# Order of loads, slots and low parts ahead of and inside the first Strassen job of a decoder layer

## The chip, the cores and the metric

The kernel runs on one core of a Trainium2 chip. The metric is the device time of one execution in microseconds; the time of a kernel is the median of its runs. One execution is also recorded by the hardware profiler, and all rows shown come from that one. Engines are named as in the profile: PE is TensorE (PEld its weight loads), DVE is VectorE, ACT is ScalarE, POOL is GpSimd, SP is SyncE, which here only issues DMAs. q1 is the DMA queue that SP issues on, q0 the one of POOL.

## The reference

One layer of a decoder trunk, 512 positions, width 2048, all in float32:

```
h = rms_norm(x)
q, kv, gates, z_a, u|v, z_b, m = split(h @ w_in)          # 2048 x 10800
o_a = sparse_attention(q, kv, gates) * silu(z_a)          # 16 heads of 64, 4 groups
o_b = gelu(u) * (tril(w_s) @ layer_norm(gelu(v)) + b_s) * silu(z_b)
x  += (sigmoid(m_a) * (o_a @ w_up_a) + sigmoid(m_b) * (o_b @ w_up_b)) @ w_out
x  += sigmoid(x @ w_ple_gate) * (p @ w_ple)
out = rms_norm(x)
```

With 512 positions the selection keeps all 8 blocks, so the selected branch is ordinary causal attention, as the window branch is.

## The kernel before

**Matmuls.** Every float32 operand is kept as two parts, a high part (rounded by a copy on ACT, function `high`, L140) and a low part (source minus high part, on DVE, `low`, L146). A product is three matmuls: high by high, high by low, low by high. The parts of h lie in `act_h` and `act_l` (16 k-tiles of 128 by 512 positions).

**Jobs.** A job (L38) is one block of output columns. All jobs form one list, and the generator `gemm` (L312) emits them one after another; `fill(n)` (L406) takes n pieces from it and `finish(name)` (L410) takes pieces until that job is done. Between pieces, other work is emitted (attention, transposes). So the order in which each engine gets its instructions is the order of this Python code, and an instruction that waits holds up those behind it on its engine.

**What runs at each step of a job.** `flush()` (L134) runs the functions in `deferred` (each may put further ones there for the next flush; `later`, L632, puts one two flushes away). `split_to` (L257) makes the high and low weight parts of the step two ahead. `pop()` (L305) takes functions from `background`, `state["pops"]` a step on average. Then come the matmuls, and at the end of a product its `evac`.

**Kinds of job.** "T" and "N" jobs are plain products; a T piece is one k-tile (three matmuls) and a step of it four k-tiles. "S" jobs use Strassen's seven products in Winograd's form on a 2 by 2 split of positions, inner dimension and columns, 2 x 512 columns at a time. Such a job has seven products of four steps; a step has twelve matmuls and four pieces. Most S jobs interleave the products in pairs. Job u (L698) runs them as 1, 2, 5, then 6 and 3 alternating, 7, 4. In the numbering of the code, product 1 needs the first half of h alone, 2 the other half, 5, 6 and 3 need sums of the quarters of h (`hsum_dram`), 7 another one (`h3_dram`, loaded over columns 256 to 511 of `act_h` and `act_l`). Products 1, 6, 7 and 4 add into the same pair of PSUM banks, 5 and 3 into a second pair, 2 has a third (`BANK_OF`, L61).

**What u leaves.** `evac_quad` (L646) copies the results of products 1, 5 and 6 into `keep` tiles on ACT (L656), adds 3, 7 and 2 to them on DVE (L667), and gives each finished quarter to `final_u` (L677: gelu in place on ACT, store by POOL). Product 4 comes from PSUM. `keep` of product 1 uses the tag s1, two slots of the pool quad.

**The stretch around u.** Ahead of it lies the attention (L1083 to L1302), in which the remaining q and za jobs (T) are spread between the attention's own work: `per_period` (L1265) pieces a slot, so that 8 pieces are left at its end. The attention's pool is then closed, and the pools quad and mix open in its place (L1307 to L1310). `load_next` (L224) lets SP ask for u's weights. The rest of za7 follows; its gating (`evac_za`, L530) uses a temporary tile of mix, tag v. Then come, in this order: POOL's loads of the sums for product 3 and of h3 (L1323 to L1328); SP's loads of the spatial-gating weights wn (tag v) and bias bn (tag s1) (L1423 to L1429); `state["pops"] = 1.15` and twelve pieces of u (L1433, L1434); the transpose of bn (L1436) and its copy; four pieces, and twice the transposes of wn, their masking (L1443) into ws (tags g0 and g1), a store and four pieces. Then the four `oa_chunk` lists go into `background`.

**The oa parts.** `oa_chunk(c)` (L1330) prepares the attention's output for the later Strassen job `w_up_a`: 13 entries, one popped at a time. Entry 0 loads two 128x512 tiles (tag v, two slots). `put` takes high and low parts of a tile into one slot each of g0 and g1 and stores them (two to four stores of 128 KB). Entries 3, 6, 9 and 12 are puts; 7 and 8 form sums in place. The chunks must be done when job vn ends, 28 steps after u.

**Keys.** The jobs k00, k01, k10, k11 (`evac_k`, L484) end with four copies on ACT (L489) and, at once, four subtractions on DVE (L491). Meanwhile sums of h are formed in the background (`h_chunk`, L436), each with a high and a low part of its own (tile h_stage).

**Slots.** A pool's tag has a fixed number of slots. A new tile waits until the last reader of the slot's former tile is done, wherever that reader stands in the code.

Of the kernel before, what the change touches and what calls it, by code (L numbers as in the profile page):

```python
# [21 lines left out]
P = 128  # L22
# [42 lines left out]
def kernel(ctx: ExitStack, tc: tile.TileContext, x, p, norm_g, w_in,  # L65
# [418 lines left out]
    def evac_k(b, a):  # L484
        def f(ps):
            g0, g1 = kk(b, 2 * a), kk(b, 2 * a + 1)
            lo_r, up_r = slice(0, 64), slice(64, 128)
            for dst, srow, g in ((lo_r, lo_r, g0), (up_r, up_r, g1), (up_r, lo_r, g0), (lo_r, up_r, g1)):
                nc.scalar.copy(ob_h[dst, g], ps[srow])  # L489
            for dst, srow, g in ((lo_r, lo_r, g0), (up_r, up_r, g1), (up_r, lo_r, g0), (lo_r, up_r, g1)):  # L490
                nc.vector.tensor_tensor(out=ob_l[dst, g], in0=ps[srow], in1=ob_h[srow, g].bitcast(F32),  # L491
                                        op=ALU.subtract)
        return f
# [151 lines left out]

    def evac_quad(final, place=None, tiles=True):  # L646

# [3 lines left out]
        def e(p, ps):  # L651
            if p in "156":
                tag, pool, bufs = {"1": ("s1", quad["pool"], 2), "5": ("hi", stream, 4), "6": ("lo", stream, 3)}[p]
                keep[p] = [pool.tile([P, 512], F32, tag=tag, name="keep" + p, bufs=bufs) for _ in range(2)]
                for t in range(2):
                    nc.scalar.copy(keep[p][t], ps[t])  # L656
            elif p in "372":
                other, row, c = {"3": ("6", 0, 512), "7": ("5", 2, 512), "2": ("1", 0, 0)}[p]
                for t in range(2):
                    o = keep[other][t]  # L660
                    if place:
                        o = place(row + t, c)
# [4 lines left out]
                    nc.vector.tensor_tensor(out=o, in0=ps[t], in1=o, op=ALU.add)  # L667
# [12 lines left out]

    def final_vn(t, c, o, src):
# [15 lines left out]

    add_job(Job("u", "S", w_in, C_UV, 512, KT, part_act, evac_quad(final_u), ("s", "g", "t"), order=("1", "2", "5", "63", "7", "4")))  # L698
    for i, (n, c, final) in enumerate((("vn", C_UV + 1024, final_vn), ("zb", C_ZB, final_zb))):
# [564 lines left out]
    n = len(slots)  # L1264
    credit, per_period = 0.0, (phase_b_units - 19 - 8) / (n + 3)  # L1265

# [43 lines left out]
    mix["pool"] = ph_mix.enter_context(tc.tile_pool(name="mix", bufs=1))  # L1310
    tmp_pool.update(p=mix["pool"], n=2, tag="v")
    load_next()
    finish("za7")
    for _ in range(2):
# [7 lines left out]

    sums_of["3"] = [new_s4(q) for q in range(2)]  # L1323
    for q in range(2):
        nc.gpsimd.dma_start(sums_of["3"][q], hsum_dram["3"][:, 4 * q:4 * q + 4])
    for i, a in enumerate((act_h, act_l)):
        for q in range(2):
            nc.gpsimd.dma_start(a(slice(4 * q, 4 * q + 4), slice(256, 512)), h3_dram[:, 4 * q:4 * q + 4, 256 * i:256 * i + 256])  # L1328

    def oa_chunk(c):  # L1330
# [7 lines left out]

        def put(n, places, sl=slice(0, 512)):

            def f():
                h, l = (mix["pool"].tile([P, S], F32R, tag=g, name="oa_" + g)[:, :sl.stop - sl.start] for g in ("g0", "g1"))
                split(h, l, w[n][:, sl], 0.5, later=True)

                def store():
# [11 lines left out]
        def sums_24():  # L1357
# [50 lines left out]
    def s4_chunk(c, new_sum=new_sum):  # L1408
# [8 lines left out]
        def second():  # L1417
# [4 lines left out]

    wn, ws = ([mix["pool"].tile([P, 4, P], F32, tag=tags[i], name=n, bufs=2 if tags == "vv" else 1) for i in range(2)]  # L1423
              for n, tags in (("wn", "vv"), ("ws", ("g0", "g1"))))
    tri = mix["pool"].tile([P, P], F32, tag="w", name="tri")
    bn = new_sum().rearrange("p a s -> p (a s)")[:8, :P]
    for hf in range(2):
        nc.sync.dma_start(wn[hf], sgu_w[4 * hf:4 * hf + 4].rearrange("g t s -> t g s"))
    nc.sync.dma_start(bn, sgu_b)  # L1429
# [385 lines left out]
```

## Time and profile before

| | |
|---|---|
| median of 3 runs | 1582.59 us (1582.2 to 1583.36) |
| the profiled execution | 1583.81 us, of which 1582.1 us is the span |
| PE busy | 1548.1 us, 98% of the span |
| DVE, ACT, POOL busy | 1194.5, 786.6, 252.6 us |
| DMA | 269.23 MB, 170 GB/s over the span |
| PE in the chain that ended last | 88% |
| granted PE clock over the execution | 0.992 |

How to read the rows. A row of a timeline has the start and the length in us, the engine, the line of the kernel, the operation, the tile written and the tile read, the shape and the count; in square brackets stands how long the engine sat idle just before and what it waited for. A row of waits has the engine, its line and what released it, then the total, the number of times and the longest. A row of stretches has the stretch, its length, then the busy time and the number of instructions for each engine, the granted clock of PE (1.00 is full), the busy share of the 16 DMA engines and GB/s. A row of DMA issues has the count, the KB of each and the median us from issue to landing.

### The profile page before, as it was taken

The numbers are of one execution on the slowest core, as the hardware profiler recorded it, in microseconds if no ns is written. First come the engines' busy times: TensorE is split into PE (matmuls) and PEld (weight loads), VectorE is DVE, ScalarE is ACT, GpSimd is POOL, SyncE is SP. The second block draws the span as 40 slices with busy tenths as digits, with TensorE's granted clock in tenths as the row PEclk, the third lists the DMA queues.
The fourth block names the chain that finished last, engine by engine and source line by source line (L and its number), as shares of the span: only waits on it lengthen the run. The fifth ranks groups of instructions, "written<-read, shape, count | busy, mean of one in ns | idle before, by whom it ended". The sixth has DMA issues, their size and how long they took to land.

```text
span 1582.1 us, 20502 instructions
## 1 busy us (share of the span) xinstructions
PE 1548.1 (98%) x7438; PEld 1292.7 (82%) x7438; DVE 1194.5 (76%) x1869; ACT 786.6 (50%) x1343; POOL 252.6 (16%) x408
## 2 busy tenths in 40 slices
PE   9999999999999889999999999999999999999997
PEld 8888988888887678888888888888888888888886
DVE  6556758879895677978887778787757587888877
ACT  6434446666663345554554444445423343544555
POOL 1201101101123123300221121211113121000100
PEclk9999999999999899999999999999999999999999
DMA  9425721113315775735473646486552369454555
GB/s 324 121 80 181 224 75 54 51 51 100 87 55 176 256 232 174 235 111 186 149 270 131 227 132 232 169 287 239 206 193 93 115 211 300 147 186 173 183 199 190
DMA packets 162309, 269.23 MB, mean 170 GB/s; under 512 B 9736, under 2 KB 81056, under 8 KB 159648
## 3 DMA queue, kind: packets, MB, share of 16 engines
q1 hardware_dynamic: 117312, 152.20, 29.6%
q0 software_dynamic: 44752, 115.47, 21.7%
q8 instruction: 58, 0.95, 0.2%
q14 instruction: 43, 0.35, 0.1%
q10 hardware_dynamic: 144, 0.26, 0.0%
HBM read 209.69 MB, written 58.20 MB: 169 GB/s over the span
## 4 chain that ended last, share of the span: by engine, by line
PE 88%; DVE 5%; DMA 2%; ACT 2%; issue 2%; POOL 1%; SPq 0%; DVEq 0%; POOLq 0%; ACTq 0%
PE ps_m L336 6%; PE ps_m L337 6%; PE ps_m L338 6%; PE ps_ub L376 2%; PE ps_wo L375 2%; PE ps_wo L376 2%; PE ps_wo L374 2%; PE ps_ub L374 2%; PE ps_ub L375 2%; PE ps_wo L337 2%; PE ps_wo L336 2%; PE ps_wo L338 2%; PE ps_pg L338 2%; PE ps_ua L338 2%; PE ps_ua L336 2%
## 5 line engine op out<-in xcount | busy, mean ns | idle before, releaser
L148 DVE TENSOR_TENSOR ls<-b,hs 128x1024 fp32r<-128x1024 f32 x196 | 239.8, 1224 | 117.6 <-ACT hs L142 116.7
L142 ACT CAST hs<-b 128x1024 fp32r<-128x1024 f32 x196 | 205.7, 1051 | 230.7 <-PE ps_m L338 86.4
L148 DVE TENSOR_TENSOR lo<-raw,hi 128x512 fp32r<-128x512 f32 (+1 forms) x216 | 151.4, 707 | 82.5 <-issue 19.7
L142 ACT CAST hi<-raw 128x512 fp32r<-128x512 f32 (+1 forms) x216 | 129.7, 608 | 137.7 <-PE ps_ub L376 48.5
L142 ACT CAST hs<-raw 128x1024 fp32r<-128x1024 f32 x80 | 84.1, 1053 | 90.1 <-PE ps_m L338 35.5
L148 DVE TENSOR_TENSOR ls<-raw,hs 128x1024 fp32r<-128x1024 f32 x80 | 97.8, 1222 | 14.9 <-ACT hs L142 14.6
L336 PE MATMUL ps_m<-hs,act_h 128*128 128x512 f32 x256 | 100.5, 392 | 0.0
L337 PE MATMUL ps_m<-ls,act_h 128*128 128x512 f32 x256 | 99.7, 389 | 0.0
L338 PE MATMUL ps_m<-hs,act_l 128*128 128x512 f32 x256 | 99.7, 389 | 0.0
L245 DVE TENSOR_TENSOR b<-b,b 128x1024 f32<-128x1024 f32 x80 | 97.5, 1218 | 1.1 <-DMA b<-in_w_in_dram 1.1
L245 DVE TENSOR_TENSOR b<-raw,b 128x1024 f32<-128x1024 f32 x80 | 97.4, 1218 | 0.0
L1112 ACT ACTIVATE prob<-prob,st 128x512 f32<-128x512 f32 (+3 forms) x128 | 70.7, 555 | 17.3 <-DVE st L1103 17.3
L142 ACT CAST pth<-ps_t 128x512 fp32r<-128x512 f32 (+1 forms) x88 | 47.7, 544 | 50.3 <-PE ps_t L1151 49.9
L148 DVE TENSOR_TENSOR ptl<-ps_t,pth 128x512 fp32r<-128x512 f32 (+1 forms) x88 | 55.7, 638 | 19.2 <-ACT pth L142 18.7
L1103 DVE CUSTOM_DVE_ANT_0 prob<-ps_s,b 128x512 f32<-128x512 f32 (+3 forms) x128 | 56.3, 486 | 6.2 <-PE ps_s L1100 5.7
L338 PEld LDWEIGHTS ps_m<-hs,act_l 128*128 128x128 f32 x256 | 48.1, 188 | 10.1
L336 PEld LDWEIGHTS ps_m<-hs,act_h 128*128 128x128 f32 x256 | 48.1, 188 | 9.8
L337 PEld LDWEIGHTS ps_m<-ls,act_h 128*128 128x128 f32 x256 | 48.1, 188 | 9.6
L362 PE MATMUL ps_za<-act_h,hi 128*128 128x512 f32 x128 | 55.0, 430 | 0.0
L362 PE MATMUL ps_q<-act_h,hi 128*128 128x512 f32 x128 | 54.0, 422 | 0.0
L1151 PEld LDWEIGHTS ps_t<-ident,prob 128*128 128x128 f32 x320 | 39.7, 140 | 13.6 <-DVE ptl L148 2.3
L364 PE MATMUL ps_za<-act_h,lo 128*128 128x512 f32 x128 | 50.4, 394 | 0.0
(635 smaller groups left out, 4406.4 us busy)
## 6 DMA issues: line engine op xcount, KB each, us to landing
raw<-in_w_in_dram SPq DMA_DIRECT2D x112, 512.0 KB, 3.6
b<-in_w_in_dram SPq DMA_DIRECT2D x56, 512.0 KB, 5.3
raw<-in_w_out_dram SPq DMA_DIRECT2D x24, 512.0 KB, 3.6
raw<-in_w_ple_gate_dram SPq DMA_DIRECT2D x24, 512.0 KB, 3.8
raw<-in_w_up_b_dram SPq DMA_DIRECT2D x16, 512.0 KB, 3.6
oa_d<-oa_g POOLq DMA_DIRECT2D x56, 128.0 KB, 2.5
hsum<-h_stage POOLq DMA_DIRECT2D x12, 512.0 KB, 3.7
gate<-keep POOLq DMA_DIRECT2D x24, 256.0 KB, 3.7
```

What stands on the lines that cost most here:

```text
L142: nc.scalar.copy(hi, src)
L148: nc.vector.tensor_tensor(out=lo, in0=src, in1=hi.bitcast(F32), op=ALU.subtract)
L245: nc.vector.tensor_tensor(out=b[o], in0=b[x], in1=b[y], op=ALU.subtract)
L336: nc.tensor.matmul(o, ah, wh, start=st, stop=False, skip_group_check=go)
L337: nc.tensor.matmul(o, ah, wl, start=False, stop=False, skip_group_check=go)
L338: nc.tensor.matmul(o, al, wh, start=False, stop=sp, skip_group_check=go)
L362: nc.tensor.matmul(ps, hi[:, j], ah, start=st, stop=False)
L374: nc.tensor.matmul(o, ah[:, sl], hi[:, j], start=st, stop=False)
L375: nc.tensor.matmul(o, ah[:, sl], lo[:, j], start=False, stop=False)
L376: nc.tensor.matmul(o, al[:, sl], hi[:, j], start=False, stop=sp)
L1103: nc.vector.tensor_tensor_reduce(out=pt[:, j * n:j * n + n], in0=o[:, j], in1=b0[:, 512 - n:], scale=-SLOPE[h], scalar=3.0e38, op0=ALU.add ...
L1112: nc.scalar.activation(sl, sl, AF.Exp, bias=st[:, 0, j, hh:hh + 1], scale=-1.0, accum_out=st[:, 1, j, hh:hh + 1])
```

## The change

1. `evac_k`: the four low parts are no longer made at once. Two are made at the next flush, two at the one after it.
2. `evac_quad` gets `then`, and u gets `u_then`: at the ends of products 1 and 2 POOL copies one column of the product's keep tile (a wait for the product), and behind it asks for the sums of product 3 (after 1) and for h3 (after 2). The loads at the old place are gone.
3. `per_period` leaves 6 pieces instead of 8 after the attention.
4. za7's temporary moves from mix (v, two slots) to quad (hs, three slots).
5. wn and bn are asked for by POOL right after u's first weights, ahead of `finish("za7")`, instead of by SP behind the loads of h3. bn stays in a slot of s1.
6. The transposes of bn and wn come after 20 pieces of u instead of 12; pops go from 1.15 to 1.25 a step.
7. `oa_chunk`: 15 entries instead of 13, puts at 5, 9, 12 and 14. The first put uses g0 and g1, the others one of them alone: the low part goes into the source tile itself or into the free half of the slot. Low parts and stores follow at the next flush, in one function.

```diff
@@ evac_k
+            todo = ((lo_r, lo_r, g0), (up_r, up_r, g1)), ((up_r, lo_r, g0), (lo_r, up_r, g1))
+            for dst, srow, g in todo[0] + todo[1]:
                 nc.scalar.copy(ob_h[dst, g], ps[srow])
-            for dst, srow, g in ((lo_r, lo_r, g0), (up_r, up_r, g1), (up_r, lo_r, g0), (lo_r, up_r, g1)):
-                nc.vector.tensor_tensor(out=ob_l[dst, g], in0=ps[srow], in1=ob_h[srow, g].bitcast(F32),
-                                        op=ALU.subtract)
+
+            def lows(i):
+                for dst, srow, g in todo[i]:
+                    nc.vector.tensor_tensor(out=ob_l[dst, g], in0=ps[srow], in1=ob_h[srow, g].bitcast(F32),
+                                            op=ALU.subtract)
+                if i == 0:
+                    deferred.append(lambda: lows(1))
+            deferred.append(lambda: lows(0))
@@ evac_quad
+                if then:
+                    then(p, keep[p][1])
...
+                if then:
+                    then(p, keep[other][1])
@@ u
+    def u_then(p, o):
+
+        if p not in "12":
+            return
+        nc.gpsimd.tensor_copy(small[:, 72:73], o[:, 0:1])
+        if p == "1":
+            sums_of["3"] = [new_s4(q) for q in range(2)]
+            for q in range(2):
+                nc.gpsimd.dma_start(sums_of["3"][q], hsum_dram["3"][:, 4 * q:4 * q + 4])
+        else:
+            for i, a in enumerate((act_h, act_l)):
+                for q in range(2):
+                    nc.gpsimd.dma_start(a(slice(4 * q, 4 * q + 4), slice(256, 512)),
+                                        h3_dram[:, 4 * q:4 * q + 4, 256 * i:256 * i + 256])
@@ attention
-    credit, per_period = 0.0, (phase_b_units - 19 - 8) / (n + 3)
+    credit, per_period = 0.0, (phase_b_units - 19 - 6) / (n + 3)
@@ ahead of u
-    tmp_pool.update(p=mix["pool"], n=2, tag="v")
+    tmp_pool.update(p=quad["pool"], n=3, tag="hs")
     load_next()
+    bn = quad["pool"].tile([P, 2, 256], F32, tag="s1", name="bn", bufs=2).rearrange("p a s -> p (a s)")[:8, :P]
+    for hf in range(2):
+        nc.gpsimd.dma_start(wn[hf], sgu_w[4 * hf:4 * hf + 4].rearrange("g t s -> t g s"))
+    nc.gpsimd.dma_start(bn, sgu_b)
     finish("za7")
...
-    for hf in range(2):
-        nc.sync.dma_start(wn[hf], sgu_w[4 * hf:4 * hf + 4].rearrange("g t s -> t g s"))
-    nc.sync.dma_start(bn, sgu_b)
...
-    state["pops"] = 1.15
-    fill(12)
+    state["pops"] = 1.25
+    fill(20)
@@ oa_chunk
+        def put(n, tags, places, sl=slice(0, 512)):
...
+                width = sl.stop - sl.start
+                h = mix["pool"].tile([P, S], F32R, tag=tags[0], name="oa_" + tags[0])
+                if len(tags) == 2:
+                    l = mix["pool"].tile([P, S], F32R, tag=tags[1], name="oa_" + tags[1])
+                else:
+                    l = w[n].bitcast(F32R) if width == 512 else h[:, 256:]
+                high(h[:, :width], w[n][:, sl], 0.5)
+
+                def rest():
+                    low(h[:, :width], l[:, :width], w[n][:, sl], 0.5)
                     for j, i in enumerate(places):
                         for a, o in enumerate((h, l)):
                             nc.gpsimd.dma_start(oa_dram[:, i, a, c], o[:, 256 * j:256 * j + 256])
-                later(store)
+                deferred.append(rest)
...
-        return [load, nothing, nothing, put("2", (5, 6)), nothing, nothing, put("1", (0,), lo_t), sums_13, sums_24,
-                put("1", (2, 4)), nothing, nothing, put("2", (3, 1))]
+        return ([load] + 4 * [nothing] + [put("2", ("g0", "g1"), (5, 6))] + 3 * [nothing]
+                + [put("1", ("g0",), (0,), lo_t), sums_13, sums_24, put("1", ("g1",), (2, 4)), nothing, put("2", ("g0",), (3, 1))])
```

More of the change, by code (lines that the diff above doesn't have):

```diff
@@ L644, in part_act, with evac_quad @@
         return sum_part(p, k, sl), sum_part(p, k, slice(t * P + 256, t * P + 256 + P))
-    def evac_quad(final, place=None, tiles=True):
+    def evac_quad(final, place=None, tiles=True, then=None):
         keep = {}
@@ L696, in final_zb @@
         deferred.append(rest)
-    add_job(Job("u", "S", w_in, C_UV, 512, KT, part_act, evac_quad(final_u), ("s", "g", "t"), order=("1", "2", "5", "63", "7", "4")))
+    add_job(Job("u", "S", w_in, C_UV, 512, KT, part_act, evac_quad(final_u, then=u_then), ("s", "g", "t"), order=("1", "2", "5", "63", "7", "4")))
     for i, (n, c, final) in enumerate((("vn", C_UV + 1024, final_vn), ("zb", C_ZB, final_zb))):
@@ L1321, in new_s4 @@
         return t
[L1323 to L1328, printed above, removed]
     def oa_chunk(c):
@@ L1421, in s4_chunk @@
         return [first, second]
[L1423 to L1426, printed above, removed]
-    for hf in range(2):
-        nc.sync.dma_start(wn[hf], sgu_w[4 * hf:4 * hf + 4].rearrange("g t s -> t g s"))
-    nc.sync.dma_start(bn, sgu_b)
     nc.gpsimd.memset(tri, 1.0)
```

8 lines of the change are left out of this document (3 added, 5 removed).

## The prediction

> **What bounds the kernel now.** I read the page first, then TensorE's waits, then the stretches around each of them.
>
> ```profile
> span 1582.1 us, 20502 instructions
> PE 1548.1 (98%) x7438; PEld 1292.7 (82%) x7438; DVE 1194.5 (76%) x1869; ACT 786.6 (50%) x1343; POOL 252.6 (16%) x408
> ```
>
> TensorE is busy 98% of the span, so 34 us of idle time is nearly all that a change of order can win. The list of TensorE's waits (total, times, longest) says where it sits:
>
> ```profile
> PE ps_u L336 <- ACT hs L142: 6.1, 1, 6.1
> PE ps_u L336 <- DVE keep L667: 4.7, 1, 4.7
> PE ps_b L1436 <- DMA sum<-in_sgu_b_dram: 2.4, 1, 2.4
> PE ps_k L364 <- DVE lo L148: 1.9, 1, 1.9
> ...
> PE ps_c L1253 <- DVE st L1103: 1.3, 1, 1.3
> ```
>
> Three of the four longest lie in job u, the fourth in the key jobs: the places that the change edits. The stretches around them (length, then busy time and instructions of PE, PEld, DVE, ACT, POOL, then granted clock, DMA share, GB/s) show what they really cost:
>
> ```profile
> 127.27:133.28 6.01, 4.14 (x11) 3.13 (x11) 5.15 (x9) 1.25 (x3) 1.51 (x3) 0.72 0.63 188
> 490.26:498.44 8.18, 8.18 (x38) 6.58 (x36) 1.53 (x3) 0.73 (x2) 2.41 (x4) 1.00 0.56 161
> 498.44:499.20 0.76, 0.16 (x2) 0.01 (x1) 0.02 (x1) 0.67 (x2) 0.00 (x0) 1.00 0.96 331
> 499.20:508.73 9.53, 9.06 (x36) 6.59 (x36) 6.69 (x10) 6.39 (x10) 2.04 (x3) 1.00 1.06 402
> 508.73:515.86 7.13, 4.75 (x15) 3.58 (x15) 1.80 (x3) 0.60 (x2) 4.55 (x8) 0.76 0.98 314
> 530.00:534.00 4.00, 4.00 (x19) 3.34 (x18) 1.90 (x2) 0.00 (x0) 0.00 (x0) 1.00 1.25 386
> 535.89:546.41 10.52, 3.98 (x10) 2.69 (x10) 6.14 (x6) 6.21 (x8) 3.74 (x7) 0.68 0.38 118
> 546.41:579.97 33.56, 33.56 (x149) 27.59 (x147) 27.30 (x30) 17.83 (x22) 9.59 (x18) 1.00 0.58 154
> 579.97:590.81 10.84, 6.12 (x16) 4.75 (x16) 7.69 (x11) 2.70 (x4) 1.63 (x3) 0.69 1.06 375
> 210.00:490.00 280.00, 275.14 (x1537) 231.61 (x1536) 233.12 (x695) 180.60 (x481) 42.72 (x70) 1.00 0.21 63
> ```
>
> The undisturbed stretch gives the pace: 33.56 us for 148 starts (one of the 149 runs in from before), 0.227 us a matmul, 2.72 us for a product of twelve. Taking off the one or two instructions that run in, each stall costs its stretch less what its own matmuls need:
>
> - K, keys: 6.01 - 10 x 0.227 = **3.7**
> - B, transpose of the gating bias: 7.13 - 12 x 0.227 - 0.1 = **4.3**
> - C, early in the product 5/6: 10.52 - 8 x 0.227 = **8.7**
> - D, between products 7 and 4: 10.84 - 14 x 0.227 = **7.7**
>
> These are far above the bare waits (1.9, 2.4, 6.1, 4.7), because the granted clock of those stretches is 0.68 to 0.76. A wait of 1.9 us was enough for that; the attention stretch, 210 to 490, holds waits up to 1.3 us and keeps 1.00. I put the point in between.
>
> **The change, part by part.** I count u's steps of 2.72 us from 0: product 1 is steps 0 to 3, 2 is 4 to 7, 5 is 8 to 11, 6 and 3 alternate in 12 to 19, 7 is 20 to 23, 4 is 24 to 27. Weights are split two steps ahead. With u starting at 500.6 on this trace's clock (below) and 1.4 us of small waits and transposes, step n starts near 502 + 2.72 n.
>
> *Keys.*
>
> ```profile
> 122.14 2.36 ACT L489 CAST ob_h<-ps_k 64x512 fp32r<-64x512 f32 x4
> 124.54 2.80 DVE L491 TENSOR_TENSOR ob_l<-ps_k,ob_h 64x512 fp32r<-64x512 f32 x4 [3.08 <-ACT ob_h L489]
> 127.35 0.69 DVE L148 TENSOR_TENSOR h_stage<-h,h_stage 128x512 fp32r<-128x512 f32 x1
> 127.96 0.69 DVE L148 TENSOR_TENSOR h_stage<-h_a,h_stage 128x512 fp32r<-128x512 f32 x1
> 128.56 1.29 DVE L148 TENSOR_TENSOR lo<-raw,hi 128x512 fp32r<-128x512 f32 x2
> 129.30 0.50 PE L364 MATMUL ps_k<-act_h,lo 128*128 128x512 f32 x1 [1.87 <-DVE lo L148]
> ```
>
> VectorE idles 3.08 us for the copies, does four low parts and two h_stage parts (4.0 us) and only then the weights' lo, which TensorE awaits. Nothing is added or removed: the four become two and two, one flush later each, behind the h_stage parts, which then run inside the 3.08 us. New order: h_stage to about 123.5, two low parts (1.4) to 124.9, lo at 125.0 to 125.7, wanted at 127.3. The other two low parts come a sub-step later, 1.4 us of DVE work against 1.6 us of slack. I take **-3.7**; the ends are that and 0.
>
> *Start of u.* The attention's fill gets 2 more units (-8 becomes -6), so 2 fewer are left after it.
>
> ```profile
> 492.18 1.23 POOL L1188 TENSOR_TENSOR o<-o,oc 128x256 f32<-128x256 f32 x1 [1.79 <-DVE o L1187]
> 493.44 2.12 SPq L220 DMA_DIRECT2D b<-in_w_in_dram  x4
> 498.99 4.21 SPq L1428 DMA_DIRECT2D wn<-in_sgu_w_dram  x2
> 503.25 2.03 SPq L1429 DMA_DIRECT2D sum<-in_sgu_b_dram  x1
> 498.53 1.14 ACT L142 CAST hi<-b 128x512 fp32r<-128x512 f32 x2 [7.32 <-DMA b<-in_w_in_dram]
> ```
>
> u's first weights can be asked for only when the attention's last GpSimd add ends at 493.4 and frees its memory; they arrive at 498.5, and TensorE, which has 36 matmuls to cover this (490.26 to 498.44), already idles 0.76. Six matmuls fewer of cover is 1.36 us: this edit **loses**. The idle time becomes 2.1 us, above the 1.9 that lowered the clock in K; half of K's cost (1.9) was that. Part falls beside the wait for the second weights, so I take 1.2. Together **+2.6**, between +1.4 (no drop) and +3.3. [...]
>
> *Gating weights and bias (B).* Three DMAs move from SP, behind the weight loads and a wait for zt's slot (4.2 and 2.0 us on SP), to GpSimd ahead of za7's end. GpSimd issues one in about 0.55 us (the pair for oa_f, quoted below, took 1.08), so 1.7 us come ahead of za7's gating product, which needs za7's last matmul anyway. za7's temporary takes one of three hs slots instead; hs is first wanted at step 4. Asked at about 498 instead of 503 to 505, they have until step 5, about 515, and TensorE's wait goes: -4.3. The cost: bn now holds one of the two s1 slots until its transpose after step 4, but the copies of product 1 want two after step 3. ScalarE stands there for a step, and hs of step 6 follows: copy 0.6, hs 1.05, ls 1.2 after the start of step 5 make 2.9 against 2.72. I take +0.3, between 0 and 2.7 (a whole step). **-4.0**.
>
> *Sums and first attention parts (C).*
>
> ```profile
> 510.23 1.51 POOL L1328 DMA_DIRECT2D act_h<-h_d  x2
> 511.70 1.52 POOL L1328 DMA_DIRECT2D act_l<-h_d  x2
> 521.26 1.08 POOL L1337 DMA_DIRECT2D oa_f<-o_d  x2
> 538.04 0.63 ACT L144 ACTIVATE oa_g<-oa_f 128x512 fp32r<-128x512 f32 x1 [9.02 <-DMA oa_f<-o_d]
> s<-hsum POOLq DMA_DIRECT2D x2, 1024.0 KB, 9.0
> act_l<-h_d POOLq DMA_DIRECT2D x2, 512.0 KB, 22.3
> ```
>
> 4 MB of sums go out at once near 510, oa_f stands behind them for 16.8 us, and ScalarE stands 9.02 us at the first oa copy with hs of step 11 queued behind it. Afterwards sums 3 (2 MB) go out after product 1's copies, about 517 with the slot wait, and are wanted at step 13, 537. h3 (2 MB) goes out after product 2, about 526, wanted at step 20, 556. oa_f is asked for at step 8, behind h3: issues end near 530, and 2.6 MB at 386 GB/s (the stretch from 530, where they went out before) are 6.8 us from 526, so it is there at 533 to 537. Its first copy moves from step 8 to step 12 (five entries at 1.25 a step), about 536, and hs of step 15, behind it, may start as late as 541. Two GpSimd copies of one column are added, each waiting for a product's copy. Behind them on GpSimd stand the sums themselves, ws and oa_f; gelu, in place on the same tile, waits for the second, and has till step 11 (hs of that step is behind it). Both cost nothing while GpSimd is as idle as here (16%); uncovered, a copy costs what it holds up, below. **-8.7**; ends 0 and -8.7.
>
> *Slots of the oa parts (D).*
>
> ```profile
> 579.74 0.39 PE L338 MATMUL ps_u<-hs,act_l 128*128 128x512 f32 x1
> 580.61 0.42 DVE L150 SCALAR_TENSOR_TENSOR oa_g<-oa_f,oa_g 128x256 fp32r<-128x256 f32 x1 [2.64 <-DMA oa_d<-oa_g]
> 580.95 1.22 DVE L245 TENSOR_TENSOR b<-raw,b 128x1024 f32<-128x1024 f32 x1
> 583.22 0.88 DVE L419 TENSOR_TENSOR oa_f<-oa_f 128x256 f32<-128x256 f32 x2
> 584.01 1.28 DVE L667 TENSOR_TENSOR keep<-ps_u,keep 128x512 f32<-128x512 f32 x2
> ```
>
> Product 4 adds onto product 7's bank, so its first matmul awaits the adds, which stood behind a low part that waited 2.64 us for a store out of its slot. Now each slot rests 4 entries or more (8.7 us) instead of 3, and at 1.25 a step the low parts of chunk 0 end in step 20; step 23 holds only empty entries. But the adds can't start before product 7 ends: 0.64 for the first and about 0.3 for two hand-overs leave 1.0 us (too short for the clock). 7.7 - 1.0: **-6.7**; ends -6.9 and 0. In chunk 1 the load waits for a store in place (oa_f is its own low part), four steps (10.9 us) before its copy is due, and the copy itself may slip 4 us (hs, as in C); GpSimd has only u's stores behind that wait.
>
> The sum is -3.7 + 2.6 - 4.0 - 8.7 - 6.7 = **-20.5 us**. The profiled execution took 1583.81 us (span 1582.1 and 1.7 around it), 1.2 above the median of 1582.59; it would take 1563.3, and the median **1562.1**.
>
> **Rivals.**
> [...]
> 2. *The wait moves instead of going.* If oa_f needs 16.8 us again from 528.5, it lands at 545.3, 4.3 us past 541, and a lowered clock adds 2.5: 1569. For it: the engines were full until 534 before (1.25). Against: only h3's 2 MB stand ahead of it.
> 3. *The keys don't gain*, the lo still stands behind the low parts: 1565.8.
> 4. *wn delays the first weights.* The engines are full then (1.06 and 402 GB/s); 512 KB let in ahead cost 1.3 us: 1563.4. [...] Against: load_sums goes ahead of wn, and the second weights need no more than now.
> 5. *The change doesn't do what it says*: the waits come back one by one in vn, where the oa parts now run to its last step: about 1582.
> 6. *Slower: h3, asked for 14 us later, is late at step 20.* Its longest landing is 22.3 us; asked at 526 it has until 556. It turns the result over only if it lands 20.5 + 3.2 us past that, at 580, 54 us after being asked: 1586 and up. For it: the 4 MB near 510 took that long with the weights beside them. Against it: 2 MB alone, and a DMA share of 0.58 in u's later stretch.
>
> **How the numbers follow.** Chances: forecast 0.42, rival 1 0.22, 2 0.16, 3 0.06, 4 0.06, 5 0.03, 6 0.05. The low end, 1558.5, is rival 1 without B's 0.3, with D at -6.9 and with 1.9 won in the attention's small waits (1.3 and less each), whose order shifts with the fill. The high end, 1570, takes in rival 2 with one more microsecond; above lie a slot wait of a whole step beside rival 2, and rivals 5 and 6. A measurement of this kernel can tell 0.2% (3.2 us) from no change; only 5 (same) and 6 (slower) aren't faster by that: 0.92 faster, 0.03 same, 0.05 slower.
>
> **What would show it.** Right: no wait of ps_k above 0.5; ps_b's wait gone; ps_u waiting for hs nowhere above 1 us; one wait for keep of about 1 us; the first ps_u wait grown to about 2.1 us with a clock under 1.00 behind it; u from its first matmul to its last 18 to 19 us shorter. Wrong: the oa_g copy still waiting for oa_f beyond step 15, a wait in vn that wasn't there, the adds still behind a store, or product 6 waiting for hs longer than a step.

## The result, and the profile after

The changed kernel takes 1565.45 us in the median (1565.17 to 1568.02), beside 1582.39 us (1582.13 to 1583.36) for the kernel before on the same chip: a ratio of 0.9895, 95% interval 0.9878 to 0.9913, or 16.9 us less. The forecast was 1562.1 with a range of 1558.5 to 1570. The profiled execution took 1565.66 us; its page begins

```profile
span 1564.0 us, 20519 instructions
PE 1541.5 (99%) x7438; PEld 1287.1 (82%) x7438; DVE 1193.2 (76%) x1869; ACT 786.5 (50%) x1343; POOL 257.3 (16%) x413
```

Of the 18.1 us that the span lost, TensorE's idle time gave 11.5 and its busy time 6.6, though it runs the same 7438 matmuls: the waits that went had each left some microseconds at a lowered clock behind them (0.68 to 0.76 in their stretches; granted clock over the execution 0.992 before, 0.998 after). TensorE's waits in the changed kernel (total, times, longest):

```profile
PE ps_u L336 <- ACT hi L142: 2.4, 2, 1.6
PE ps_c L1268 <- DVE st L1128: 1.9, 2, 1.5
PE ps_u L337 <- DVE ls L148: 1.5, 2, 0.8
PE ps_spin L926 <- POOL eps_t L87: 1.4, 1, 1.4
PE ps_u L336 <- DVE keep L675: 1.3, 1, 1.3
PE ps_pg L337 <- DVE ls L148: 1.0, 2, 0.8
```

The waits of 6.1, 2.4 and 1.9 us are gone, and that of 4.7 is down to 1.3; the longest left in u is 1.6, at its start. The stretches of the keys, of u's start and of products 7 and 4 all run at full clock (length, then busy time and instructions of PE, PEld, DVE, ACT, POOL, then clock, DMA share, GB/s):

```profile
122.00:127.50 5.50, 5.50 (x26) 4.36 (x25) 3.68 (x7) 3.40 (x7) 1.08 (x2) 1.00 1.03 365
495.10:502.90 7.80, 6.31 (x24) 4.46 (x25) 4.66 (x7) 4.16 (x8) 2.63 (x5) 1.00 1.06 403
560.00:575.00 15.00, 13.73 (x61) 11.04 (x60) 13.79 (x15) 7.20 (x9) 5.23 (x10) 1.00 0.97 311
```

**Where the time went.** The table compares the two traces by the starts of TensorE's rows: each figure is the time from the first matmul of a stage to the first of the next.

| stage | term | before | after | difference | forecast |
|---|---|---|---|---|---|
| up to job q (keys in it) | K | 185.91 | 181.25 | -4.66 | -3.7 |
| attention, to za7's last matmul | | 312.30 | 312.13 | -0.17 | 0 |
| za7's last matmul to u's first, less one matmul | A | 0.76 | 1.78 | +1.02 | |
| u, steps 0 and 1 | A | 6.81 | 7.62 | +0.81 | +2.6 with the row above |
| u, steps 2 to 7 | B | 21.72 | 17.74 | -3.98 | -4.0 |
| u, steps 8 to 11 | C | 19.59 | 11.85 | -7.74 | -8.7 |
| u, steps 12 to 19 | C | 21.76 | 22.89 | +1.13 | 0 |
| u, end of step 22 to step 25 | D | 15.84 | 9.71 | -6.13 | -6.7 |
| vn | | 76.66 | 75.93 | -0.73 | 0 |
| last gate jobs (ps_pg) | | 164.82 | 167.59 | +2.77 | 0 |

Up to the end of vn the rows add up to -20.5 us, the forecast's sum, though the single rows miss it by up to 2.1. Then 2.8 us are given back, more than 700 us later, in jobs that the diff doesn't touch; the stages between differ by 0.1 together, and what follows the gate jobs is 0.35 shorter, which makes up the 18.1 of the span.

**Keys.** VectorE's timeline in the changed kernel:

```profile
122.06 0.69 DVE L148 TENSOR_TENSOR h_stage<-h_a,h_stage 128x512 fp32r<-128x512 f32 x1
124.45 1.39 DVE L494 TENSOR_TENSOR ob_l<-ps_k,ob_h 64x512 fp32r<-64x512 f32 x2 [1.70 <-ACT ob_h L490]
125.87 0.69 DVE L148 TENSOR_TENSOR lo<-raw,hi 128x512 fp32r<-128x512 f32 x1
126.59 1.39 DVE L494 TENSOR_TENSOR ob_l<-ps_k,ob_h 64x512 fp32r<-64x512 f32 x2
```

The h_stage part runs ahead of the copies' end, the lo stands behind two low parts instead of four, and two follow it. TensorE has no wait left here.

**Start of u.** TensorE's timeline:

```profile
493.38 0.39 PE L364 MATMUL ps_za<-act_h,lo 128*128 128x512 f32 x1
495.39 0.49 PE L336 MATMUL ps_u<-hi,act_h 128*128 128x512 f32 x1 [1.63 <-ACT hi L142]
...
499.65 0.51 PE L336 MATMUL ps_u<-hi,act_h 128*128 128x512 f32 x1 [0.74 <-ACT hi L142]
```

The wait grew as forecast (0.60 to 1.63), but the matmuls from the third on start 0.23 us apart: no lowered clock. Instead the second weights are waited for, 0.74 (e11 shows what made them late).

**Sums and first parts.** GpSimd, ScalarE and TensorE in the changed kernel, in the order of time:

```profile
511.53 0.59 ACT L662 COPY keep<-ps_u 128x512 f32<-128x512 f32 x1 [2.96 <-PE ps_b L1460]
512.18 0.18 POOL L695 COPY small<-keep 128x1 f32<-128x1 f32 x1 [11.71 <-ACT keep L662]
523.66 3.39 POOL L695 COPY small<-keep 128x1 f32<-128x1 f32 x1 [2.68 <-DVE keep L675]
527.08 0.63 ACT L688 ACTIVATE keep<-keep 128x512 f32<-128x512 f32 x1 [2.71 <-POOL small L695]
529.95 1.15 POOL L1362 DMA_DIRECT2D oa_f<-o_d  x2
529.96 0.51 PE L337 MATMUL ps_u<-ls,ob_h 128*128 128x512 f32 x1 [0.66 <-DVE ls L148]
538.29 0.63 ACT L144 ACTIVATE oa_g<-oa_f 128x512 fp32r<-128x512 f32 x1 [3.96 <-DMA oa_f<-o_d]
541.98 0.50 PE L337 MATMUL ps_u<-ls,s 128*128 128x512 f32 x1 [0.83 <-DVE ls L148]
```

The 6.07 us wait is gone. What is left of it is 0.66 in step 11, behind a one-column copy that took 3.39 us where its twin took 0.18, and 0.83 in step 15, behind an oa_f that landed at 538.3.

**Products 7 and 4.** VectorE adds directly at the product's end, and TensorE waits only for the add:

```profile
566.97 1.28 DVE L675 TENSOR_TENSOR keep<-ps_u,keep 128x512 f32<-128x512 f32 x2
567.80 0.47 PE L336 MATMUL ps_u<-hs,act_h 128*128 128x512 f32 x1 [1.27 <-DVE keep L675]
```

**The end.** In the last gate jobs stands one new wait, and a second of 0.20 six microseconds ahead of it:

```profile
1506.82 0.50 PE L337 MATMUL ps_pg<-ls,act_h 128*128 128x512 f32 x1 [0.77 <-DVE ls L148]
```

The diff shows no reason for it, but the code has one: `pop` (L305) adds `state["pops"]` a step to the counter `state["due"]` and takes a function whenever it reaches 1. Jobs u, vn and zb have 84 steps; 84 x 1.15 = 96.6 leaves 0.6 in the counter, 84 x 1.25 = 105.0 leaves nothing. Nothing resets it, so from there on every function of the background falls on another step.

### The profile page after: what moved, and what is told of

Its sections match the earlier page's. It is cut to its first block, busy times and chain, and to the rows that moved or that the text cites. A ratio compares the mean times of both kernels' runs of the same rounds, so it can differ in the third digit from the quotient of the medians.

```text
span 1564.0 us, 20519 instructions
## 1 busy us (share of the span) xinstructions
PE 1541.5 (99%) x7438; PEld 1287.1 (82%) x7438; DVE 1193.2 (76%) x1869; ACT 786.5 (50%) x1343; POOL 257.3 (16%) x413
## 4 chain that ended last, share of the span: by engine, by line
PE 86%; DVE 6%; issue 3%; ACT 2%; DMA 2%; POOL 1%; DVEq 0%; SPq 0%; POOLq 0%; ACTq 0%
PE ps_m L336 7%; PE ps_m L337 7%; PE ps_m L338 7%; PE ps_wo L376 2%; PE ps_ub L376 2%; PE ps_ub L375 2%; PE ps_wo L374 2%; PE ps_wo L375 2%; PE ps_ub L374 2%; PE ps_wo L337 2%; PE ps_wo L338 2%; PE ps_ua L338 2%; PE ps_zb L338 2%; PE ps_zb L337 2%; PE ps_vn L338 2%
## 5 line engine op out<-in xcount | busy, mean ns | idle before, releaser
L1137 ACT ACTIVATE prob<-prob,st 128x512 f32<-128x512 f32 (+3 forms) x128 | 70.7, 555 | 15.9 <-DVE st L1128 15.9
L364 PE MATMUL ps_za<-act_h,lo 128*128 128x512 f32 x128 | 50.4, 394 | 0.0
L364 PE MATMUL ps_q<-act_h,lo 128*128 128x512 f32 x128 | 50.4, 394 | 0.0
```

The costliest lines, as they stand in the source:

```text
L364: nc.tensor.matmul(ps, lo[:, j], ah, start=False, stop=sp)
L1137: nc.scalar.activation(sl, sl, AF.Exp, bias=st[:, 0, j, hh:hh + 1], scale=-1.0, accum_out=st[:, 1, j, hh:hh + 1])
```

## The experiments

The theory after the result: five local causes as forecast, with the places of the requests and puts as what decides, and a sixth, the carried fraction. Eleven kernels tested it. The stages that nine of them moved by more than half a microsecond are in this table (worked out as above, us; the columns are the labels of the experiments without their second half); e2 and e7, which start from the kernel before, are told below:

| | before | after | e1 | e3 | e4 | e5 | e6 | e9 | e10 | e11 | e8 |
|---|---|---|---|---|---|---|---|---|---|---|---|
| wait ahead of u | 0.76 | 1.78 | 1.75 | 0.74 | 1.85 | 1.79 | 1.73 | 1.78 | 1.92 | 1.77 | 0.84 |
| u steps 0, 1 | 6.81 | 7.62 | 7.46 | 7.95 | 7.71 | 7.79 | 7.88 | 7.41 | 7.70 | 7.67 | 7.64 |
| 2, 3 | 10.20 | 5.44 | 5.44 | 5.44 | 5.44 | 5.44 | 5.44 | 5.44 | 6.21 | 5.44 | 5.44 |
| 4 to 7 | 11.52 | 12.30 | 12.30 | 12.29 | 16.12 | 12.30 | 12.30 | 12.29 | 11.52 | 12.29 | 12.29 |
| 8 to 11 | 19.59 | 11.85 | 11.84 | 11.83 | 10.92 | 10.88 | 11.84 | 11.85 | 10.88 | 11.85 | 10.88 |
| 12 to 19 | 21.76 | 22.89 | 22.92 | 22.27 | 21.76 | 21.76 | 22.54 | 30.04 | 21.76 | 23.15 | 21.76 |
| 23 to 25 | 15.84 | 9.71 | 9.70 | 9.71 | 9.71 | 9.70 | 9.86 | 16.04 | 9.70 | 9.72 | 9.67 |
| zb | 75.93 | 75.93 | 75.94 | 75.93 | 75.94 | 75.94 | 81.07 | 75.94 | 75.94 | 75.93 | 75.93 |
| last gate jobs | 164.82 | 167.59 | 165.86 | 167.04 | 168.98 | 167.41 | 170.39 | 167.25 | 167.39 | 167.80 | 164.86 |

Several variants differ from the changed kernel by 1 to 2 us, and there the intervals of the times overlap; the stages of their traces carry those verdicts. How well a stage repeats is seen in e7, which is the kernel before up to the end of zb. Its stages without a long wait agree with that kernel's to 0.15 us. Those with one do not: the keys took 1.24 us less, steps 2 to 7 1.09 less, steps 8 to 11 1.36 more, steps 23 to 25 1.17 less and vn 1.43 more. So a difference against the one trace of the kernel before is good to a microsecond or so in these rows, while in the changed kernel and its variants the rows without a wait repeat to 0.1 us.

### The keys alone (e2)

The kernel before with the change's edit of `evac_k`, quoted in the change above, and nothing else.

> The kernel before with the keys' low parts deferred, and nothing else. Theory: the wait of ps_k for lo (1.87 us) goes and the clock stays at 1.00 there; u starts 4.4 to 4.7 us earlier, 1578.0 to 1578.6 where the kernel before has 1582.4 to 1583.3. Rival (the lo's come no earlier; the changed kernel gained there by something else): no wait less, within 1 us of before.

Measured: 1579.54 us beside 1583.6, ratio 0.9976, interval 0.9967 to 0.9985. The wait of ps_k is gone, job q starts 4.7 us earlier, and the wait of ps_b is there as before (2.29 us). So K is a gain of its own, of about 4 us, somewhat less than the 4.4 to 4.7 expected.

### The carried fraction, from both sides (e1, e7)

```diff
     finish("zb")
     assert not background
+    state["due"] = 0.5999999999999925
```

That is e1, on the changed kernel. e7 sets 0.0 at the same place of the kernel before.

> The changed kernel, with one number set: after job zb the carried fraction of the pop counter is 0.6, as the kernel before has it there (the changed kernel carries 0.0, since 84 steps at 1.25 leave another rest than 84 at 1.15). Theory (carried fraction): the 2.8 us that the changed kernel loses in the last gate jobs come from it; from the first to the last ps_pg matmul it takes 164.8 us again in place of 167.6, and the kernel 1562.7. Rival (chance of that execution, DMA timing): nothing moves, 167.6 and 1565.4.

> The kernel before, with the fraction that the counter of pops carries out of job zb set from 0.6 to 0.0, as the change leaves it; nothing else. If the carried fraction is what costs the change its time in the last gate jobs, the stretch from the first to the last matmul of ps_pg grows here from 164.8 us to 167 to 168, and the time by 2 to 2.8 us, to about 1585. If the later start or the other slots of the change do that, ps_pg stays within 0.3 us of 164.8 and the time within 0.5 us.

Measured: e1 1563.68 us, ratio 0.988 (0.9863 to 0.9896), the last gate jobs at 165.86 instead of 167.59, so 1.7 of the 2.8 us come back. e7 1586.53 beside 1582.55, ratio 1.0023 (1.0013 to 1.0033), the last gate jobs at 170.06 instead of 164.82. e7 lost more than expected, because there a longer wait came, with seven matmuls at a lowered clock behind it (their starts 0.42 to 0.43 us apart, 0.23 at full clock):

```profile
1554.60 0.50 PE L392 MATMUL ps_pg<-tl,ob_l 128*128 128x512 f32 x1 [1.09 <-DVE tl L148]
```

Of all thirteen kernels of this study, the four that carry 0.6 (before, e1, e2, e8) spend 164.8 to 165.9 us here, the nine that carry 0.0 spend 167.0 to 170.4. The fraction is the cause. Its price is not fixed: among the nine the order of the work is the same from there on, and what differs is which waits came about in that execution.

### The cover at u's start (e3)

```diff
-    credit, per_period = 0.0, (phase_b_units - 19 - 6) / (n + 3)
+    credit, per_period = 0.0, (phase_b_units - 19 - 8) / (n + 3)
```

> The changed kernel with 8 pieces left after the attention instead of 6. Theory (cover): the first wait of ps_u falls from 1.63 to about 0.8 and u starts 0.9 to 1.3 us earlier relative to the end of za7, 1564.1 to 1564.6. Rival (wn, now ahead of the weights' later part on the other queue, delays the first weights): the wait stays at 1.4 to 1.7 and the time at 1565.4.

Measured: 1564.48 us, ratio 0.9884 (0.9869 to 0.9898). The wait ahead of u fell by 1.04 us and steps 0 and 1 grew by 0.33: the two units cost what they no longer cover, less what then stands beside the second weights' landing. Steps 0 and 1 stay 1.1 us above the kernel before (7.95 against 6.81), so that part of A is not the fill's.

### The requests for sums and h3 at the old place (e4)

```diff
-    add_job(Job("u", "S", w_in, C_UV, 512, KT, part_act, evac_quad(final_u, then=u_then), ("s", "g", "t"), order=("1", "2", "5", "63", "7", "4")))
+    add_job(Job("u", "S", w_in, C_UV, 512, KT, part_act, evac_quad(final_u), ("s", "g", "t"), order=("1", "2", "5", "63", "7", "4")))
...
+    sums_of["3"] = [new_s4(q) for q in range(2)]
+    for q in range(2):
+        nc.gpsimd.dma_start(sums_of["3"][q], hsum_dram["3"][:, 4 * q:4 * q + 4])
+    for i, a in enumerate((act_h, act_l)):
+        for q in range(2):
+            nc.gpsimd.dma_start(a(slice(4 * q, 4 * q + 4), slice(256, 512)), h3_dram[:, 4 * q:4 * q + 4, 256 * i:256 * i + 256])
```

> The changed kernel with the sums of product 3 and h3 asked for at the old place, before u, and without the two GpSimd copies; all else as changed. Theory (the place of the first put does it): the 7.7 us of stall C stay away, because the first oa copy comes at step 12 instead of 8; the GpSimd copy of 3.4 us is gone and oa_f is asked for earlier, so the two small waits at steps 11 and 15 (2.1 us together) go too; the 4 MB beside the first weights may cost up to 1.5 at steps 1 to 8: 1563.4 to 1565.5. Rival (the asks do it): oa_f stands behind 4 MB again and ScalarE with it, 5 to 9 us of wait for hs come back with a lowered clock, 1570 to 1574.

Measured: 1568.65 us, ratio 0.9908 (0.9893 to 0.9923). C did not come back: steps 8 to 19 are even clean. The loss, 3.8 us where up to 1.5 was allowed for it, sits in steps 4 to 7, in rows of TensorE, ScalarE and VectorE:

```profile
515.66 1.05 ACT L142 CAST hs<-raw 128x1024 fp32r<-128x1024 f32 x1 [2.70 <-DMA raw<-in_w_in_dram]
517.83 1.22 DVE L245 TENSOR_TENSOR b<-b,b 128x1024 f32<-128x1024 f32 x1 [3.54 <-DMA b<-in_w_in_dram]
520.25 0.50 PE L337 MATMUL ps_u<-ls,act_h 128*128 128x512 f32 x1 [1.99 <-DVE ls L148]
```

4 MB on GpSimd's queue land beside u's weights. The rows of the DMA issues (KB each, median us to landing) show it on the h3 loads, first the changed kernel's, then this one's:

```profile
act_h<-h_d POOLq DMA_DIRECT2D x2, 512.0 KB, 4.8
act_l<-h_d POOLq DMA_DIRECT2D x2, 512.0 KB, 7.4
```

```profile
act_h<-h_d POOLq DMA_DIRECT2D x2, 512.0 KB, 14.3
act_l<-h_d POOLq DMA_DIRECT2D x2, 512.0 KB, 21.1
```

So the later requests do not win C. They keep the weights of steps 4 to 7 on time. The kernel before had the requests at this same place and took 11.52 us for these steps; it reached them after B's stall of 4.8 us. That the stall gave the weights their time is argued, not tried.

### Both requests behind product 1 (e5)

```diff
-        if p not in "12":
+        if p != "1":
             return
         nc.gpsimd.tensor_copy(small[:, 72:73], o[:, 0:1])
-        if p == "1":
-            sums_of["3"] = [new_s4(q) for q in range(2)]
+        sums_of["3"] = [new_s4(q) for q in range(2)]
...
-        else:
-            for i, a in enumerate((act_h, act_l)):
+        for i, a in enumerate((act_h, act_l)):
...
```

> The changed kernel with both asks behind the one GpSimd copy after product 1; no copy after product 2. Theory (the second copy costs): ScalarE's 2.7 us wait for that copy and the 0.66 us wait at step 11 go, oa_f no longer comes at 538, and the wait at step 15 goes: 2 us less, 1563.4. Rival (bandwidth): 4 MB at once beside the weights of products 5 and 6 make the weights late, waits for ls or hs of 1 to 4 us at steps 6 to 11, 1566 to 1569.

Measured: 1563.66 us, ratio 0.9881 (0.9866 to 0.9896). Without the second copy, and with h3 and oa_f asked earlier, steps 8 to 11 get 0.97 us shorter and steps 12 to 19 get 1.13 shorter: the two rests of C. ScalarE still stands 2.96 us for the s1 slot here, as in the changed kernel, and it costs nothing.

### Old slots and later stores (e6)

```diff
-        def put(n, tags, places, sl=slice(0, 512)):
+        def put(n, places, sl=slice(0, 512)):
...
+                h, l = (mix["pool"].tile([P, S], F32R, tag=g, name="oa_" + g)[:, :sl.stop - sl.start] for g in ("g0", "g1"))
+                split(h, l, w[n][:, sl], 0.5, later=True)
...
+                later(store)
```

The entries stay where the change puts them.

> The changed kernel with the oa parts' slots and stores as before (a high and a low part in g0 and g1 for every put, stores two flushes later, no part in place), at the new entries 5, 9, 12 and 14. Theory (slots): with puts 2 and 3 entries apart the high and low parts wait for stores again, 2 us and more each, and hs or the adds behind them: steps 20 to 26 of u take 20 to 23 us instead of 17.9, 1567 to 1571. Rival (the entries suffice: step 23 holds none): 17.9 and 1565.4.

Measured: 1572.38 us, ratio 0.9933 (0.992 to 0.9945). D did not return; the wait for the add is 1.46 us instead of 1.27. Slots or stores (they were undone together) matter at another place, the start of zb:

```profile
567.75 0.47 PE L336 MATMUL ps_u<-hs,act_h 128*128 128x512 f32 x1 [1.46 <-DVE keep L675]
662.67 0.51 PE L336 MATMUL ps_zb<-hs,act_h 128*128 128x512 f32 x1 [2.19 <-ACT hs L142]
```

That wait has eight matmuls at a lowered clock behind it and costs 5.1 us; the last gate jobs lost 2.8 more.

### The first put three entries earlier (e9)

```diff
-        return ([load] + 4 * [nothing] + [put("2", ("g0", "g1"), (5, 6))] + 3 * [nothing]
+        return ([load] + [nothing] + [put("2", ("g0", "g1"), (5, 6))] + 6 * [nothing]
```

> The changed kernel with the first put of each chunk at entry 2 instead of 5 (step 10 of u for the first). Theory (place of the first put): ScalarE stands there until oa_f lands at about 538, hs of step 13 comes 4.5 us late, the clock falls, and steps 12 to 20 take 5 to 7 us more than now: 1570 to 1572. Rival (with the asks as changed oa_f would be in time anyway): within 1 us of 1565.4.

Measured: 1579.8 us, ratio 0.9976 (0.9966 to 0.9986). That is 8 to 10 us above what was expected, because two stalls came instead of one. Steps 12 to 19 take 7.2 us more and steps 23 to 25 take 6.3 more: C and D are both back. TensorE, and ScalarE ahead of the second wait:

```profile
539.68 0.76 PE L336 MATMUL ps_u<-hs,s 128*128 128x512 f32 x1 [4.42 <-issue]
574.45 0.63 ACT L144 ACTIVATE oa_g<-oa_f 128x512 fp32r<-128x512 f32 x1 [4.99 <-DMA oa_f<-o_d]
578.82 0.77 PE L336 MATMUL ps_u<-hs,act_h 128*128 128x512 f32 x1 [5.36 <-DVE keep L675]
```

In chunk 0 the copy waits 8.15 us for oa_f, in chunk 1 4.99; hs stands behind it on ScalarE, and in chunk 1 the add behind the low part on VectorE. One list of entries, shifted by three, undoes 13.5 of the 17 us.

### The two halves of B (e10, e11)

```diff
 e10
-    fill(20)
+    fill(12)
     b = bank("o", "ps_b")
...
+    fill(8)
     for c in range(4):
         background.extend(oa_chunk(c))
 e11
-    for hf in range(2):
-        nc.gpsimd.dma_start(wn[hf], sgu_w[4 * hf:4 * hf + 4].rearrange("g t s -> t g s"))
-    nc.gpsimd.dma_start(bn, sgu_b)
     finish("za7")
...
+    for hf in range(2):
+        nc.sync.dma_start(wn[hf], sgu_w[4 * hf:4 * hf + 4].rearrange("g t s -> t g s"))
+    nc.sync.dma_start(bn, sgu_b)
     nc.gpsimd.memset(tri, 1.0)
```

> The changed kernel with the transposes of bias and weights back after 12 and 16 pieces of u instead of 20 and 24 (the oa lists still enter the background at the changed place); bias and weights are asked for early, as in the changed kernel. Theory, it is the early request that took the wait of ps_b: the bias has landed before u starts, so there is no wait of ps_b, steps 2 and 3 take 5.4 us, and the time stays within 1 us of the changed kernel's. Rival, it is the later place: the wait of ps_b comes back with some 2 us and steps 2 and 3 take 9 to 10 us, time 1569.

> The changed kernel with bias and weights of the gating asked for by SP at the old place again, behind u's first two steps of weights; the transposes stay after 20 and 24 pieces. Theory, the early request took the wait: SP stands some 4 to 6 us at the requests as before, the bias lands near 510, about when the transpose after step 4 is due (513), so ps_b waits under 0.5 us, but the weights of the third to fifth step are asked for 4 to 6 us later and TensorE waits for them at step 4 or 5 with a lowered clock: 2 to 4 us slower, 1567.5 to 1569.5. Rival, the later place alone would have done: no wait in steps 2 to 7 and the time within 1 us of the changed kernel's.

Measured: e10 1563.61 us, ratio 0.9882 (0.9869 to 0.9896); e11 1565.63, ratio 0.9892 (0.9879 to 0.9906), the changed kernel's time. Neither has a wait of ps_b: each half alone removes it. For e11 the theory falls and its rival holds. SP no longer stands for za7's tile, but its request for bn is out 12.0 us after the first one for u's weights, no sooner than in the kernel before (11.8). What differs is that the transpose comes 9.9 us behind that request instead of 6.0:

```profile
495.06 3.42 SPq L1452 DMA_DIRECT2D wn<-in_sgu_w_dram  x2
498.53 2.77 SPq L1453 DMA_DIRECT2D bn<-in_sgu_b_dram  x1
```

The move of za7's temporary was not undone in any run.

e11 also shows what made u's second weights late. ScalarE's first high parts of them, in the changed kernel and then in e11:

```profile
498.98 1.14 ACT L142 CAST hi<-b 128x512 fp32r<-128x512 f32 x2 [2.62 <-DMA b<-in_w_in_dram]
```

```profile
497.96 1.14 ACT L142 CAST hi<-b 128x512 fp32r<-128x512 f32 x2 [1.76 <-DMA b<-in_w_in_dram]
```

SP asked for u's first weights at 489.47 and 489.31, so these parts start 9.51 and 8.65 us later. In the nine kernels in which GpSimd asks for wn and bn right behind that first request, it is 9.30 to 9.63 us; in the four in which SP asks for them behind the weights (before, e2, e7, e11), 8.54 to 8.79. The first weights' own parts start after 5.04 to 5.39 us in all of them. So the early request hardly touches the first weights and delays the second by 0.5 to 1.1 us. In e11 TensorE had nothing from it, since the clock fell behind its first wait (0.50 over 496.5 to 499.5; 7.67 us for steps 0 and 1); whether it would gain at full clock wasn't tried.

e10 gained where no change was expected: with the transposes back at their early place u is 2.1 us shorter over steps 2 to 19 (50.4 against 52.5; by the table's rows +0.77, -0.78, -0.97, -1.13). The bias gives its s1 slot back before product 1 ends, ScalarE does not stand 2.96 us (the transposes of wn came earlier with the bias's, so the slot is not tried alone), and the second copy on GpSimd, the request of oa_f and its first copy come 2.0, 5.1 and 4.9 us earlier:

```profile
521.62 0.19 POOL L695 COPY small<-keep 128x1 f32<-128x1 f32 x1 [7.58 <-DVE keep L675]
524.82 1.16 POOL L1362 DMA_DIRECT2D oa_f<-o_d  x2
533.41 0.63 ACT L144 ACTIVATE oa_g<-oa_f 128x512 fp32r<-128x512 f32 x1 [0.27 <-DMA oa_f<-o_d]
```

### The gains together (e8)

The changed kernel with e1's, e3's and e5's edits.

> The changed kernel with three edits together: the carried fraction 0.6 after zb, 8 pieces left after the attention, both asks behind the copy after product 1. If the gains add up as the single runs showed them (1.7 in the last jobs, 1.0 at u's start, 2.1 at steps 8 to 20), the last ps_pg matmul comes at 1549.2 instead of 1554.0 and the kernel takes 1560.4 to 1561. If the earlier asks meet the first weights, steps 0 to 8 take 1 to 3 us more.

Measured: **1560.12 us** (1559.87 to 1560.79), ratio 0.9854 (0.984 to 0.9867): the best version, 5.3 us below the changed kernel. The longest of TensorE's waits in u:

```profile
PE ps_u L336 <- ACT hi L142: 1.4, 2, 0.8
...
PE ps_u L336 <- ACT hs L142: 1.3, 1, 1.3
```

No wait of ps_pg of 0.2 us or more is left in it, and the last gate jobs take 164.86.

## Why the prediction was right, point by point

**K** was right in mechanism and order of work (1.4 us of low parts ahead of the lo, which starts 0.9 us later than reckoned), and a microsecond too small: -4.7 in the trace, -4.1 in e2's medians. The excess is within what one execution decides: in e7 the same wait of 1.89 us left the clock at 1.00, and the keys took 1.24 us less.

**A**, +2.6, came as +1.8, and only the wait, +1.0 of it, by the mechanism that was forecast. The wait was forecast to the third of a microsecond, the lowered clock behind it was not there, nor the 1.2 us that the sum takes for it: what the chances call rival 1, for this execution. But the price is not what a lowered clock decides. In e5 the same wait of 1.63 us did lower it, as the stretch just behind shows, first the changed kernel, then e5:

```profile
496.50:499.50 3.00, 2.41 (x11) 1.65 (x9) 0.86 (x2) 0.52 (x1) 1.73 (x3) 1.00 1.05 401
```

```profile
496.50:499.50 3.00, 3.00 (x10) 2.33 (x9) 0.81 (x2) 0.53 (x2) 1.77 (x3) 0.63 1.04 398
```

Steps 0 and 1 took 7.62 without and 7.79 with the drop: it ran beside the 0.74 us in which the second weights were late anyway. The step that failed is "so I take 1.2": nearly all of it was covered, and what came in its place, +0.8 in steps 0 and 1, is the second weights' lateness, which the early request for wn and bn explains (e11) and the sum did not have.

**B** came to the digit, -3.98 against -4.0, by luck: in e7, where the same wait of 2.44 us left full clock, the stage took 20.63 us before instead of 21.72. And the price that the step put beside it, "+0.3" for the s1 slot, was wrong. The slot wait cost TensorE nothing in product 2. Its cost fell later: ScalarE stood for the slot, VectorE stood 5.50 us for ScalarE's hs and ran behind from there, so the add of product 2 came about 2 us late, and with it GpSimd's copy, h3's requests and oa_f's. e10 is without all of it, 2.1 us; so is e5, which keeps the wait for the slot and leaves out the second copy, so it takes both to cost anything. The working put B's gain on the earlier request; e10 and e11 show that either half would have done.

**C**, -8.7, came as -6.6. The place of the first put is the mechanism, as e9 shows; the later requests for sums, which the text named beside it, are not, as e4 shows. The 2.1 us that are missing are two statements that failed. "Both cost nothing while GpSimd is as idle as here": the second copy was held up 3.2 us though GpSimd had nothing else to do, and gelu and hs behind it cost TensorE 0.97 in step 11. And "so it is there at 533 to 537": asked at 529.95, after that copy, oa_f came at 538.3, and step 15 lost 1.13. Both take B's slot and the second copy together: they are gone in e10 and in e5.

**D** has the right size, -6.1 against -6.7, and the residual wait of 1.27 instead of 1.0. The reason given, that each slot rests longer, falls with e6. What counts is that at the end of product 7 no copy or low part of the oa entries is waiting; e9 brings D back with the new slots, by a put whose load has not landed. Whether the list alone or the pops of 1.25 a step put the entries there wasn't tried apart.

**The end** was not foreseen. The step that failed is that an edit of the pops a step was followed only through u. The sum up to there was -20.5, as forecast, but that is luck: C gave 2.1 less than forecast and D 0.6 less, against 1.0 more from K, 0.8 from A and 0.9 from the attention and vn, for which nothing was forecast. One of the prediction's own signs shows it: u from its first matmul to its last is 15.9 us shorter (99.10 to 83.18), not 18 to 19. The 2.8 us beyond the sum are more than the 2.4 by which the profiled execution (1565.66) stands above the forecast for it (1563.3).

**The rivals.** 2: oa_f was late again, but by 0.8 us of TensorE's time and not with a drop of the clock; in e11, where it came 0.15 us later still, the wait was 1.09. 3: ruled out by e2. 4: ruled out for the first weights by e11, where wn goes out 4.6 us later and u starts no sooner (wait 1.77 against 1.78); for the second weights it holds, and "the second weights need no more than now" was the wrong argument against it. 5: not here, but e9 shows how near it lies. 6: no wait at step 20 in any kernel.

## What to carry to other kernels

Read a stall by its stretch, with the matmuls that it should hold taken off: here each stage came within 2.1 us of its forecast even where the reason was wrong, and a sum that fits better than its terms fits by cancelling. Only undoing one part at a time tells which part did it. Where an instruction holds up its engine while it waits for a load, what decided here is the place at which it stands in that engine's order, so move the place first and buy slots after; and a tile borrowed from a rotating tag is paid for by whoever needs the slot next, here several queues away. A pacing counter that carries a fraction must be reset, or kept, at the end of the stage that an edit is meant for, or the edit reorders everything behind it.

## What the runs showed of the hardware that had not been expected

**A one-column copy on GpSimd took 3.39 us.** Its twin took 0.18. VectorE's timeline in the changed kernel beside it:

```profile
523.51 1.22 DVE L245 TENSOR_TENSOR b<-b,b 128x1024 f32<-128x1024 f32 x1
524.65 1.22 DVE L148 TENSOR_TENSOR ls<-b,hs 128x1024 fp32r<-128x1024 f32 x1
525.78 1.22 DVE L245 TENSOR_TENSOR b<-raw,b 128x1024 f32<-128x1024 f32 x1
```

The copy starts at 523.66, inside a run of three back-to-back two-input instructions, and ends at 527.05, with the run (527.00; VectorE's next instruction starts at 528.68). In e1, e3, e6, e9 and e11 it is the same, 3.38 or 3.39 us; in e10, where it starts at 521.62 while VectorE waits for a load from 521.56 to 522.24, it took 0.19. The twin, at 512.18, falls into 5.50 us in which VectorE stands, until 513.09. So the copy took 0.18 or 0.19 us while VectorE stood, and 3.4 us for its 128 numbers where it began inside that run: it lasted to the run's end, not to that of one instruction. What holds it up isn't seen in the traces.

**The same wait lowers the clock in one execution and not in another.** At u's start, waits of 1.57 to 1.76 us lowered the clock for seven or eight matmuls in e4, e5, e6, e10 and e11, and for none in the changed kernel (1.63), e1 (1.59) and e9 (1.62): over 496.5 to 499.5 it was 0.50 to 0.63 in e4, e5, e10 and e11, and 1.00 in the changed kernel and e1. Waits of 1.5 us and less mostly left it, but one of 1.37 in e6 and one of 1.09 in e7, each with one of 0.2 behind it, lowered it for seven. And longer ones left it: in the kernel before, the wait of 1.87 us for the keys and that of 2.38 for the bias each had a lowered clock behind them (0.72 and 0.76 in their stretches); in e7 the same two waits had 1.00 in the 3 us behind them.

```profile
129.63 0.50 PE L364 MATMUL ps_k<-act_h,lo 128*128 128x512 f32 x1 [1.89 <-DVE lo L148]
510.19 0.20 PE L1436 MATMUL ps_b<-ident,sum 8*128 8x8 f32 x1 [2.44 <-DMA sum<-in_sgu_b_dram]
```

The prediction's threshold between 1.3 and 1.9 us is therefore no threshold: the drop came behind a wait of 1.09 us in one execution and stayed away behind one of 2.44 in the same. What decides it isn't seen in the traces, and wasn't tried.
